# A weight gradient with seven products per pair of slices: another form of the seven products, and accumulations that open and close bank by bank

## The chip, the cores and the metric

The kernel runs on one core of a Trainium2 chip. The metric is device time in microseconds (us). Before the change, three runs gave 163.02, 163.23 and 163.38 us; the median is 163.23 us. Five engines matter here: PE multiplies matrices (PEld is its weight load), DVE (VectorE) and ACT (ScalarE) copy and add, POOL (GpSimd) issues the input transfers, and SP issues the output transfers.

## The reference

```python
batch, m, k, n = 16, 512, 1024, 768
grad_weight = np.einsum('bmk,bmn->kn', input, grad_output)   # float32, 1024 x 768
```

The sum runs over 8192 rows. The kernel cuts them into 64 slices of 128 rows. A slice of the input (128 x 1024) and the same slice of the gradient (128 x 768) give a contribution to all 1024 x 768 outputs.

## The kernel before

**Plain slices.** The output is cut into quarters A, B (input columns 0 to 511) and C, D (columns 512 to 1023), each with one half of the 768 gradient columns. A quarter has four blocks q of 128 x 384, and a block fills one PSUM bank. A plain slice takes 4 x 4 = 16 matmuls of 128 x 128 by 128 x 384.

**Pairs with seven products.** Two adjacent slices can be seen as a 2 x 2 by 2 x 2 block product, which a scheme of Strassen's kind does with seven block products in place of eight: 28 matmuls for a pair in place of 32. For it DVE forms sums and differences of the slices in bf16 first. The string `LOADS` (line 11) says which of the 32 pairs is plain (`s`) and which takes seven products (`P`): seven plain pairs first, then 23, then two plain ones.

The five functions `sum_g1`, `sum_g2`, `sum_x1`, `sum_x2`, `sum_x3` (lines 133 to 158) form the sums of a pair on 1152, 768, 1024, 512 and 1024 columns. Of the seven products two go straight to the quarters A and D; the other five (m, n, o, p, q) have accumulators of their own in `macc` (line 80). At the end `share` (line 179) adds `macc` to the quarters in `acc`: 20 operations on DVE, named by `SHARES`.

**Order of the work.** The engines' orders are written out by hand: `manual_schedule` keeps the program's order on PE, DVE, ACT and POOL. `ORDER` (line 17) lists visits to a quarter or product; a visit takes all four blocks together, in four banks (0 to 3 or 4 to 7), over some slices, and `!` closes it. When a visit opens, ACT may copy the old partial sum from SBUF back into some of its banks (`carry`, line 297). When it closes, `shut` (line 349) either lets ACT copy the bank out (line 354), for blocks that were carried or are new, or lets DVE add the bank to the sum in SBUF (line 358). A number ahead of a step, or behind its `!`, says how many operations of the list `filler` (the sums of the pairs, then the shares) DVE does there.

**Transfers.** POOL issues the loads, which turn float32 into bf16 on the way: one transfer of each operand per pair from pair 2 on (`MERGED = 2`, lines 114 and 115), one per slice before that (lines 119 and 121). 14 pairs are held in SBUF, and sums of 9 pairs. Slices 0 and 1 of the input and slice 0 of the gradient come as float32 and are rounded by DVE and ACT (`round_by`, line 212).

**The end.** The last block is multiplied in two parts, of 256 and 128 columns, in two banks (line 393), each added (line 401) and stored (line 403) by itself.

Of the kernel before, what the change touches and what calls it, by code (L numbers as in the profile page):

```python
# [9 lines left out]
P = 128  # L10

LOADS = "sssssssPPPPPPPPPPPPPPPPPPPPPPPss"
# [5 lines left out]
ORDER = (  # L18
    "A1:3!0,0,0,0 C1:1 B1:3 B2!0,0,0,0 C2!0,0,0,0 D2:3 A2 D3 A3 D4!0,0,0,0 A4 B4:1^!0,0,0,0 C4 "
    "C6!0,0,0,0 A6!0,0,0,0 D6:2~!0,0,0,0 B6:3^ C8!0,0,0,0 B8!0,0,0,0 D8:2~!0,0,0,0 A8!0,0,0,0 "  # L20
    "D9:2 B10!0,0,0,0 D10!0,0,0,0 A10 B12:2^!0,0,0,0 A12!0,0,0,0 D12:3 B14!0,0,0,0 D14!0,0,0,0 "
    "C13:3^ C14!6,0,0,0 A15:1 1o2:4!1,1,1,0 q2:4!0,1,0,1 A16!0,0,0,0 D16:1^ p3:4!2,1,1,0 "
    "D17!0,0,0,0 n3:2 1o4:3!2,0,0,1 n4!0,0,0,0 m4:4!1,1,1,2 p5:1^!0,0,0,0 A19:3^!0,0,0,1 q4:4~ "
    "2q6!2,0,1,0 D20!1,0,0,0 o7:4~!0,1,1,1 n7:2^!1,0,0,1 m7:1^!1,0,0,0 p8:1~ 2A22:4!2,1,0,2 "
    "p9!0,0,0,0 D23:3~!0,0,1,0 q9:3^ 2q10!2,0,0,0 o10:2^!1,0,0,0 n10:2^ 2n11!2,0,0,0 "
    "A25:4~!1,0,1,0 m10:2^ 2m12!2,0,0,0 D26!1,0,0,0 p13:4~!0,1,2,1 o13:3~!0,0,1,1 q12:3~ "
    "2A28:2~!2,0,0,1 q13!0,0,0,0 n15:3~!2,0,1,1 D28:1^!0,0,1,0 o16:2^!0,0,0,0 q16:2~!2,0,0,1 "
    "m15:3~ 1p17:3^!4,0,1,1 D30!1,0,0,0 m16 m18!0,0,0,0 q18:4~!1,1,0,1 A32 1n19:4^!4,0,1,2 "
    "o20:1~!0,1,0,0 D34:3^ 4D35!1,0,0,0 A35!1,0,0,0 o22:2^ p21:4 5p23!1,0,1,1 o23!0,0,0,0 q21:2~ "
    "q23!3,0,0,0 m21:4~ m23!2,1,0,0 n21:4~ A38:0-q n23!5,0,0,1 A40 B18:4!2,1,0,1 A41!0,0,0,0 "  # L30
    "C17:3 C18!1,0,0,0 D41!3,0,0,0 "
# [3 lines left out]
SHARES = (  # L35
    "l20 l21 l22 t20 t21 t22 t10 t11 t12 t13 l23 t23 l10 l11 l12 l13 l30 l31 l32 l33 "
).split()

WARMUP = [("b", 512), ("f", 512), ("f", 512), ("b", 512)]
PAIRS_HELD = 14  # L40
SUMS_HELD = 9

MERGED = 2
# [3 lines left out]
def kernel(  # L47
# [12 lines left out]
    S = B * M // P  # L60
# [4 lines left out]

    LEFT, RIGHT = slice(NH, N), slice(0, NH)
# [10 lines left out]

    acc = accp.tile([P, 2 * Q, N], f32, name="acc")

    macc = accp.tile([P, 5, Q, NH], f32, name="macc")  # L80
    SLOT = {"n": 0, "p": 1, "m": 2, "o": 3, "q": 4}
# [10 lines left out]

# [14 lines left out]
    xg = []  # L107
    for u, kind in enumerate(LOADS):
# [7 lines left out]
        for h in range(2):  # L116
            s = 2 * u + h
            if s > 0 and u < MERGED:
                nc.gpsimd.dma_start(out=gp[:, h, :], in_=G[s * P : (s + 1) * P, :])
            if s > 1 and u < MERGED:  # L120
                nc.gpsimd.dma_start(out=xp[:, h, :], in_=X[s * P : (s + 1) * P, :])
            if kind == "s":
                items.append(("s", xp[:, h, :], gp[:, h, :]))
        if kind == "P":
            items.append(("P", xp, gp))
        xg.append((xp, gp))

    opened = {}
# [4 lines left out]
    def sum_g1(i):  # L133
        _, xp, gp = items[i]
        ge = sums.tile([P, 3, NH], bf16, name="ge")
        xe = sums.tile([P, 3, KH], bf16, name="xe")
        extra[i] = (xe, ge)
        g = gp.rearrange("p m n -> p (m n)")
        nc.vector.tensor_add(out=ge.rearrange("p a n -> p (a n)"), in0=g[:, 0 : 3 * NH], in1=g[:, NH : 4 * NH])  # L139

    def sum_g2(i):
        _, xp, gp = items[i]
        g = gp.rearrange("p m (h n) -> p (m h) n", h=2)
        nc.vector.tensor_sub(out=g[:, 0::3, :], in0=g[:, 0::3, :], in1=g[:, 2:0:-1, :])  # L144

    def sum_x1(i):
        _, xp, gp = items[i]
        xe = extra[i][0]
        nc.vector.tensor_add(out=xe[:, 0:2, :].rearrange("p a k -> p (a k)"), in0=xp[:, 0, :], in1=xp[:, 1, :])  # L149

    def sum_x2(i):
        _, xp, gp = items[i]
        nc.vector.tensor_add(out=extra[i][0][:, 2, :], in0=xp[:, 0, 0:KH], in1=xp[:, 1, KH:K])  # L153

    def sum_x3(i):
        _, xp, gp = items[i]
        x = xp.rearrange("p m (h k) -> p (m h) k", h=2)
        nc.vector.tensor_sub(out=x[:, 1:3, :], in0=x[:, 1:3, :], in1=x[:, 0::3, :])  # L158

    def settled(quarter, q):  # L160
        for p, (_, banks) in opened.items():
            assert p != quarter or not (banks[q][1] and banks[q][2])
        assert not any(b == q and steps[m][1] == quarter for m, b in filled)

    SHARE_OF = {
        "t1": ("m", "o", 0),
        "t2": ("p", "q", 0),
        "t3": ("q", None, 0),  # L170
        "l1": ("n", "m", Q),
        "l2": ("p", "o", Q),
        "l3": (None, "n", Q),
    }
    taken = set()

    def share(name, q):
        left, right, row = SHARE_OF[name]
        sides = [
            (h, p)  # L180
            for h, p in enumerate((left, right))
            if p and ("ABCD"[(row > 0) * 2 + h], p) not in taken
        ]
        for h, _ in sides:
            settled("ABCD"[(row > 0) * 2 + h], q)
        if len(sides) == 2:
            a, b = SLOT[left], SLOT[right]
            dst = acc[:, row + q, :].rearrange("p (h n) -> p h n", h=2)
            src = macc[:, a : b + 1 : b - a, q, :]
        else:  # L190
            ((h, p),) = sides
            dst = acc[:, row + q, h * NH : (h + 1) * NH]
            src = macc[:, SLOT[p], q, :]
        op = nc.vector.tensor_sub if name[1] == "3" else nc.vector.tensor_add
        op(out=dst, in0=dst, in1=src)  # L195

    filler = []
    for i, item in enumerate(items):
        if item[0] == "P":
            filler += [(f, i) for f in (sum_g1, sum_g2, sum_x1, sum_x2, sum_x3)]  # L200
    filler += [(partial(share, c[:2]), int(c[2:])) for c in SHARES]
    filler.reverse()

    def fill(n):
        for _ in range(n):
            f, i = filler.pop()
            f(i)


    def round_by(engine, dst, src, c0, c1):  # L210
# [4 lines left out]
    round_by("DVE", g0, gf, NH, NH + 192)  # L215
    round_by("ACT", g0, gf, NH + 192, N)
# [4 lines left out]
    round_by("ACT", x0, xf[0], 6 * P, 8 * P)  # L221


    KINDS = {"A": "sP", "B": "s", "C": "s", "D": "sP"}
    streams = {
        p: [i for i, item in enumerate(items) if item[0] in KINDS.get(p, "P")] for p in "ABCDmnopq"
    }

    def operands(p, i, q):
        kind, x, g = items[i]  # L230
        k = slice(q * P, (q + 1) * P)
        k2 = slice(KH + q * P, KH + (q + 1) * P)
        left, right = LEFT, RIGHT
        if kind == "s":
            return x[:, k if p in "AB" else k2], g[:, left if p in "AC" else right]
        xe, ge = extra[i]
        return {
            "m": lambda: (xe[:, 2, k], ge[:, 1, :]),
            "n": lambda: (xe[:, 1, k], g[:, 0, left]),
            "o": lambda: (x[:, 0, k], g[:, 0, right]),  # L240
            "p": lambda: (x[:, 1, k2], g[:, 1, left]),
            "q": lambda: (xe[:, 0, k], g[:, 1, right]),
            "D": lambda: (x[:, 0, k2], ge[:, 0, :]),
            "A": lambda: (x[:, 1, k], ge[:, 2, :]),
        }[p]()

    def sum_of(p, q):
        if p in SLOT:
            return macc[:, SLOT[p], q, :]
        row = q if p in "AB" else Q + q  # L250
        return acc[:, row, 0:NH] if p in "AC" else acc[:, row, NH:N]

    done = {p: 0 for p in streams}
    fresh = {p: True for p in streams}
    slots = [0, 1]
    used = set()
# [3 lines left out]
    def parsed(step):  # L260
        step, _, ahead = step.partition("!")
        step, _, byact = step.partition(":")
        early = byact[-1:] if byact[-1:] in ("^", "~") else ""
        byact = byact.rstrip("^~")
        at = next(c for c in step if c.isalpha())
        before, upto = step.split(at)
        ahead = [int(a) for a in ahead.split(",")] if ahead else None
        return int(before or 0), at, int(upto), int(byact[:1] or 0), byact[1:], early, ahead

    steps = [parsed(step) for step in ORDER]  # L270


    def follower(n, free):
        now = {p for p in opened if p != steps[n][1]}
        shut_since = {steps[n][1]}
        for m in range(n + 1, len(steps)):
            _, p, _, byact, first, early, ahead = steps[m]
            if p not in now:
                if not free:
                    if not early:  # L280
                        return None
                    assert byact and not first and not fresh[p] and p not in shut_since
                    return m
                free -= 1
# [168 lines left out]
```

## Time and profile before

| what | us |
|---|---|
| median of three runs | 163.23 |
| span of the profiled execution, first to last instruction | 161.1 |
| PE busy | 157.0 |
| DVE busy | 140.7 |
| ACT busy | 117.9 |
| first matmul of the slices starts | 5.00 |
| last DVE addition ends | 158.1 |

The profile gives no time for its execution but the span; the median of the runs is 2.1 us longer than the span, and this remainder (launch, and landing of the last store) lies around it. PE's granted clock is full in all of the span. The busy time of an engine is the union of its instructions' durations; instructions of DVE and ACT overlap a little, so an engine's pace is read from one start to the next. In the profile's groups, a line like "L358 DVE TENSOR_TENSOR acc<-bank,acc" names the source line, the engine, what is written and read, the count, the busy time and the mean duration of one.

### The profile page before, as it was taken

Reading aid. Unit: us, or ns where it says so; the run is one execution under the profiler, and the core shown is the slowest. Engines: PE = TensorE matmul, PEld = TensorE weight load, DVE = VectorE, ACT = ScalarE, POOL = GpSimd, SP = SyncE. Lnnn points to the kernel's source line nnn. Section 1 sums busy time; section 2 is a strip of 40 time slices with the busy share of each in tenths; the row PEclk is TensorE's granted clock in tenths of the full one; section 3 lists DMA queues with packets and bytes.
Section 4 is the critical chain, followed back from the end, with each engine's and each line's share of the span. In section 5 each row is a group of like instructions: output and inputs, shape, how many; then the busy total and the mean of one; then the engine's idle time right before and its main releaser. Section 6 shows DMA issues by size and latency. Waiting matters only on the chain.

```text
span 161.1 us, 2769 instructions
## 1 busy us (share of the span) xinstructions
PE 157.0 (97%) x944; PEld 92.7 (58%) x944; DVE 140.7 (87%) x267; ACT 117.9 (73%) x278; POOL 34.8 (22%) x69
## 2 busy tenths in 40 slices
PE   8999999999999999999999999999999999999991
PEld 3365665556555565556655665556655665555561
DVE  0645888889799999999998999999989998999982
ACT  3735357545589899978998897997795667988730
POOL 7442222122222212222212222221222100000000
PEclk9999999999999999999999999999999999999999
DMA  5999999999999999999999999999999999900695
GB/s 176 297 210 214 213 214 216 212 215 212 214 213 212 212 212 216 212 213 211 214 212 217 212 215 213 213 213 213 213 212 213 213 214 213 202 21 0 239 354 191
DMA packets 12398, 33.40 MB, mean 207 GB/s; under 512 B 1376, under 2 KB 4192, under 8 KB 12384
## 3 DMA queue, kind: packets, MB, share of 16 engines
q0 software_dynamic: 9360, 28.64, 89.8%
q1 hardware_dynamic: 2592, 3.47, 6.2%
q10 hardware_dynamic: 432, 1.11, 1.8%
q8 instruction: 7, 0.11, 0.3%
q14 instruction: 7, 0.06, 0.1%
HBM read 58.72 MB, written 3.15 MB: 384 GB/s over the span
## 4 chain that ended last, share of the span: by engine, by line
PE 97%; DVE 0%; issue 0%
PE bank L338 94%; PE bank L97 3%; PE bank L393 0%; DVE acc L401 0%
## 5 line engine op out<-in xcount | busy, mean ns | idle before, releaser
L338 PEld LDWEIGHTS <-xp 128*128 128x128 bf16 x650 | 63.3, 98 | 44.4 <-DVE xp L212 1.5
L338 PE MATMUL bank<-gp,xp 128*128 128x384 bf16 x468 | 81.0, 327 | 0.0
L354 ACT COPY macc<-bank 128x384 f32<-128x384 f32 x91 | 39.3, 491 | 9.8 <-PE bank L338 9.4
L358 DVE TENSOR_TENSOR acc<-bank,acc 128x384 f32<-128x384 f32 x80 | 39.6, 550 | 5.2 <-PE bank L338 4.8
L338 PEld LDWEIGHTS <-xe 128*128 128x128 bf16 x276 | 26.9, 98 | 17.9 <-DVE xe L149 0.2
L354 ACT COPY acc<-bank 128x384 f32<-128x384 f32 x57 | 24.7, 484 | 13.9 <-PE bank L338 13.9
L297 ACT COPY bank<-macc 128x384 f32<-128x384 f32 x73 | 33.0, 493 | 1.6 <-DVE acc L358 0.9
L338 PE MATMUL bank<-ge,xp 128*128 128x384 bf16 x182 | 33.5, 326 | 0.0
L338 PE MATMUL bank<-gp,xe 128*128 128x384 bf16 x184 | 32.4, 326 | 0.0
L297 ACT COPY bank<-acc 128x384 f32<-128x384 f32 x47 | 21.5, 491 | 8.7 <-DVE acc L358 7.0
L115 POOL DMA_DIRECT2D xp<-in_input_dram x30 | 16.0, 532 | 52.1 <-DMA xp<-in_input_dram 28.9
L114 POOL DMA_DIRECT2D gp<-in_grad_output_dram x30 | 16.0, 533 | 38.1 <-PE bank L338 17.2
L358 DVE TENSOR_TENSOR macc<-bank,macc 128x384 f32<-128x384 f32 x35 | 18.0, 550 | 0.8 <-PE bank L338 0.8
L139 DVE TENSOR_TENSOR ge<-gp 128x1152 bf16<-128x1152 bf16 x23 | 17.3, 752 | 0.6 <-DMA gp<-in_grad_output_dram 0.5
L149 DVE TENSOR_TENSOR xe<-xp 128x1024 bf16<-128x1024 bf16 x23 | 15.8, 685 | 2.1 <-DMA xp<-in_input_dram 2.1
L195 DVE TENSOR_TENSOR acc<-acc,macc 128x768 f32<-128x768 f32 (+1 forms) x20 | 16.1, 871 | 0.0
L338 PE MATMUL bank<-ge,xe 128*128 128x384 bf16 x92 | 15.9, 326 | 0.0
L158 DVE TENSOR_TENSOR xp<-xp 128x1024 bf16<-128x1024 bf16 x23 | 15.7, 684 | 0.0
L144 DVE TENSOR_TENSOR gp<-gp 128x768 bf16<-128x768 bf16 x23 | 12.7, 554 | 0.5
L153 DVE TENSOR_TENSOR xe<-xp 128x512 bf16<-128x512 bf16 x23 | 9.6, 418 | 0.0
L356 DVE COPY acc<-bank 128x384 f32<-128x384 f32 x6 | 3.2, 555 | 3.2 <-PE bank L338 3.1
L212 DVE CAST gp<-gf 128x192 bf16<-128x192 f32 (+1 forms) x2 | 0.7, 330 | 4.3 <-DMA gf<-in_grad_output_dram 4.3
(20 smaller groups left out, 19.9 us busy)
## 6 DMA issues: line engine op xcount, KB each, us to landing
xp<-in_input_dram POOLq DMA_DIRECT2D x30, 512.0 KB, 16.8
gp<-in_grad_output_dram POOLq DMA_DIRECT2D x30, 384.0 KB, 16.7
out_dram<-acc SPq DMA_DIRECT2D x15, 192.0 KB, 2.4
xf<-in_input_dram ACTq DMA_DIRECT2D x2, 512.0 KB, 4.8
gp<-in_grad_output_dram POOLq DMA_DIRECT2D x3, 192.0 KB, 6.4
xp<-in_input_dram POOLq DMA_DIRECT2D x2, 256.0 KB, 7.7
gf<-in_grad_output_dram SPq DMA_DIRECT2D x2, 192.0 KB, 4.2
out_dram<-acc SPq DMA_DIRECT2D x1, 128.0 KB, 1.9
```

Source lines behind the costliest of these rows:

```text
L114: nc.gpsimd.dma_start(out=gp, in_=G[rows, :].rearrange("(p m) n -> p m n", m=2))
L115: nc.gpsimd.dma_start(out=xp, in_=X[rows, :].rearrange("(p m) k -> p m k", m=2))
L139: nc.vector.tensor_add(out=ge.rearrange("p a n -> p (a n)"), in0=g[:, 0 : 3 * NH], in1=g[:, NH : 4 * NH])
L144: nc.vector.tensor_sub(out=g[:, 0::3, :], in0=g[:, 0::3, :], in1=g[:, 2:0:-1, :])
L149: nc.vector.tensor_add(out=xe[:, 0:2, :].rearrange("p a k -> p (a k)"), in0=xp[:, 0, :], in1=xp[:, 1, :])
L153: nc.vector.tensor_add(out=extra[i][0][:, 2, :], in0=xp[:, 0, 0:KH], in1=xp[:, 1, KH:K])
L158: nc.vector.tensor_sub(out=x[:, 1:3, :], in0=x[:, 1:3, :], in1=x[:, 0::3, :])
L195: op(out=dst, in0=dst, in1=src)
L297: nc.scalar.copy(out=bank, in_=sum_of(p, q))
L338: nc.tensor.matmul(bank, stat, mov, start=opening and j == 0 and not carried, stop=close and j == len(items_now) - 1, skip_group_check=car ...
L354: nc.scalar.copy(out=dst, in_=bank)
L358: nc.vector.tensor_add(out=dst, in0=bank, in1=dst)
```

## The change

- `LOADS`: six plain pairs, then 25 pairs with seven products, then one plain pair.
- The form of the seven products: the sums of a pair are chained. For the input, stage 0 writes two differences (1024 columns), stage 1 takes one of them less a raw half (512), stage 2 adds another raw half to that (512, in place). The gradient has the like on 768, 384 and 384 columns. One product of a pair goes straight to each of A, B and C; four (1, 5, 6, 7) have accumulators in `macc`.
- `SHARES` and `share` go. The accumulators are added as the last blocks close (`close`): 6 takes 1, 7 takes 6, 5 is used twice, and A, B, C and D take one accumulator each, all on DVE from the bank.
- `ORDER` is replaced by `PLAN`, whose unit is one block, not four: `A2@1.3` multiplies block 2 of A over 3 more items, opening bank 1; `f` lets ACT copy the old sum into a bank; `c` closes a block with ACT's copy; `v` closes it with DVE, by an addition or, if the bank was filled, a copy; `x0.6` or `g2.6` is a stage of pair 6's sums.
- Blocks 0 and 1 of A and of C keep banks 0, 3, 4 and 5 from the first slice to the end. All other blocks take turns in banks 1, 2, 6 and 7.
- `MERGED = 3`: slices 4 and 5 are loaded by single transfers. `SUMS_HELD` goes from 9 to 10.

The instruction orders count: 930 matmuls of the slices, 918 of them of 384 columns and 12 parts (before: 938, 926 and 12); on DVE 137 additions of 384 columns from a bank, 24 copies from a bank and 4 + 4 closings of product 5 (before: 115, 8 and none); on ACT 105 copies out of a bank and 124 + 2 into one (before: 148 and 120 + 4).

```diff
-LOADS = "sssssssPPPPPPPPPPPPPPPPPPPPPPPss"
+LOADS = "ssssssPPPPPPPPPPPPPPPPPPPPPPPPPs"
...
+PLAN = (
+    "A0@0.1 A2@1.1 A3@2.1 A1@3.1 vA2 C2@6.1 cA3 C3@7.1 C0@4.1 r0 cC2 C1@5.1 vC3 B0@1.1 B1@2.1 B2@6.1 cB0 "
...
+    "11@1.2 c13 g0.28 11.2 53@7.4 f60@6 v11 70@2.1 g1.28 f61@1 70.3 v53 60.1 g2.28 60.3 v70 61.2 x0.28 "
...
+    "51.5 v73 f53@2 fC3@5 70.3 v51 fD1@0 53.3 fB1@6 C3.3 v70 f50@3 C0.2 v53 fD3@1 B1.7 vC3 fB3@2 50.4 vC0 "
+    "vB1 B3.4 v50 fD0@4 72.1 fB0@5 D1.2 D3.2 vB3 B0.7 v72 f52@3 fC2@6 vD1 52.4 vD3 vB0 C2.6 v52 fD2@0 "
+    "fB2@1+2 D0.2 vC2 D2.2 B2.6 vD0 vD2 vB2 "
 ).split()
-SUMS_HELD = 9
-MERGED = 2
+SUMS_HELD = 10
+MERGED = 3
...
-    macc = accp.tile([P, 5, Q, NH], f32, name="macc")
-    SLOT = {"n": 0, "p": 1, "m": 2, "o": 3, "q": 4}
+    macc = accp.tile([P, 4, Q, NH], f32, name="macc")
+    SLOT = {"1": 0, "5": 1, "6": 2, "7": 3}
...
+    def sum_x(stage, u):
+        x = tiles[u][0].rearrange("p m (h k) -> p (m h) k", h=2)
+        xe = sums_of(u)[0]
+        if stage == 0:
+            nc.vector.tensor_sub(out=xe[:, 0:2, :], in0=x[:, 1::-1, :], in1=x[:, 3::-2, :])
+        elif stage == 1:
+            nc.vector.tensor_sub(out=xe[:, 2, :], in0=xe[:, 0, :], in1=x[:, 0, :])
+        else:
+            nc.vector.tensor_add(out=x[:, 1, :], in0=x[:, 2, :], in1=xe[:, 2, :])
+
+    def sum_g(stage, u):
+        g = tiles[u][1].rearrange("p m (h n) -> p (m h) n", h=2)
+        ge = sums_of(u)[1]
+        if stage == 0:
+            nc.vector.tensor_add(out=ge[:, 0:2, :], in0=g[:, 0:2, :], in1=g[:, 1::2, :])
+        elif stage == 1:
+            nc.vector.tensor_add(out=ge[:, 2, :], in0=g[:, 3, :], in1=ge[:, 0, :])
+        else:
+            nc.vector.tensor_add(out=g[:, 1, :], in0=ge[:, 2, :], in1=g[:, 2, :])
...
+            "B": lambda: (x[:, 1, k], g[:, 3, :]),
+            "C": lambda: (x[:, 3, k], g[:, 1, :]),
+            "5": lambda: (xe[:, 0, k], ge[:, 0, :]),
+            "6": lambda: (xe[:, 2, k], ge[:, 2, :]),
+            "7": lambda: (xe[:, 1, k], ge[:, 1, :]),
...
+    SHARED = {"A": "1", "B": "5", "C": "7", "D": "6", "6": "1", "7": "6"}
...
+    def fill(p, q, b, b2):
...
+        for tile_, c0, c1 in parts:
+            nc.scalar.copy(out=tile_[:, 0 : c1 - c0], in_=src[:, c0:c1])
+        opened[p, q] = (parts, True)
...
+    def close(engine, p, q):
+        parts, carried = opened.pop((p, q))
+        final = done[p, q] == len(streams[p])
+        dst = sum_of(p, q)
+        if final and p not in "1":
...
+                if p == "5":
+                    nc.vector.tensor_sub(out=dst, in0=b, in1=sum_of("6", q))
+                    nc.vector.tensor_sub(out=sum_of("6", q), in0=b, in1=sum_of("7", q))
                 else:
+                    nc.vector.tensor_add(out=dst[:, c0:c1], in0=b, in1=sum_of(SHARED[p], q)[:, c0:c1])
+                if p in "ABCD":
...
+                    store.dma_start(out=OUT[:, row, at : at + c1 - c0], in_=dst[:, c0:c1])
...
+            if engine == "c":
+                nc.scalar.copy(out=dst, in_=b)
+            elif carried or fresh[p, q]:
+                nc.vector.tensor_copy(out=dst, in_=b)
             else:
+                nc.vector.tensor_add(out=dst, in0=b, in1=dst)
```

## The prediction

> **What bounds the kernel now.** The first view is the busy time of each engine, with the slices of the span under it.
>
> ```profile
> PE 157.0 (97%) x944; PEld 92.7 (58%) x944; DVE 140.7 (87%) x267; ACT 117.9 (73%) x278; POOL 34.8 (22%) x69
> ...
> PE   8999999999999999999999999999999999999991
> ...
> DVE  0645888889799999999998999999989998999982
> ACT  3735357545589899978998897997795667988730
> ...
> PEclk9999999999999999999999999999999999999999
> DMA  5999999999999999999999999999999999900695
> ```
>
> PE works without a hole at full clock, so time is matmuls times their pace. But DVE is full in most slices too, and the transfers are full until about slice 35 of 40: three resources run side by side with little air. The chain of the work that ended last confirms PE and gives its pace:
>
> ```profile
> 0.78 4.42 PE bank L97 x6
> 5.20 2.25 PE bank L338 x12
> 7.45 0.01 issue
> 7.46 149.34 PE bank L338 x914
> ...
> 156.79 0.67 PE bank L393 x6
> 157.46 0.02 issue
> 157.49 0.63 DVE acc L401 x2
> ```
>
> 914 matmuls in 149.34 us are 0.163 us each. The end is PE's last part and two additions, to 158.12; the store follows.
>
> The third view is DVE's timeline in a full stretch, since its durations overlap: the pace is read from start to start.
>
> ```profile
> 59.43 0.75 DVE L139 TENSOR_TENSOR ge<-gp 128x1152 bf16<-128x1152 bf16 x1
> 60.21 0.56 DVE L144 TENSOR_TENSOR gp<-gp 128x768 bf16<-128x768 bf16 x1
> 60.69 0.68 DVE L149 TENSOR_TENSOR xe<-xp 128x1024 bf16<-128x1024 bf16 x1
> 61.29 0.42 DVE L153 TENSOR_TENSOR xe<-xp 128x512 bf16<-128x512 bf16 x1
> 61.62 0.68 DVE L158 TENSOR_TENSOR xp<-xp 128x1024 bf16<-128x1024 bf16 x1
> 62.23 0.75 DVE L139 TENSOR_TENSOR ge<-gp 128x1152 bf16<-128x1152 bf16 x1
> 63.01 0.56 DVE L144 TENSOR_TENSOR gp<-gp 128x768 bf16<-128x768 bf16 x1
> 63.49 1.95 DVE L358 TENSOR_TENSOR acc<-bank,acc 128x384 f32<-128x384 f32 x4
> ```
>
> Paces: 768 columns of bf16 0.48 us, 1024 0.60, 512 0.33; an addition from a bank (1.95 - 0.55) / 3 = 0.467. An operation usually starts 0.08 before the one ahead ends (60.69 + 0.68 against 61.29), but L144, which overwrites what L139 reads, starts 0.03 after its end: a dependent operation directly behind its producer loses 0.11.
>
> **The change, part by part.**
>
> *Matmuls.* Before: 926 of 384 columns and the last block's 12 parts, worth 932; after: 918 and 12 parts, worth 924. Two more pairs with seven products save 4 each: 8 x 0.163 = **-1.30 us**, on the path.
>
> *DVE, in total.* The sums of a pair cost 0.78 + 0.48 + 0.60 + 0.33 + 0.61 = 2.80 before. After: 1024, 512, 512, 768, 384 and 384 columns, 0.60 + 0.33 + 0.33 + 0.48 + 2 x 0.27 = 2.28. The 384 form is in no row; it lies between 0.27 (the line through 512 and 1024 columns, 0.33 - 0.067) and 0.33 (as 512). I take 0.27, since 768 columns fit the same line (0.47 against 0.48). 23 x 2.80 = 64.4 becomes 25 x 2.28 = 57.0: -7.4. The shares go (16 x 0.87 + 4 x 0.47, from 0.951 and 0.550 less the overlap): -15.8. Closings with 384 columns go from 115 + 8 to 137 + 24 + 8 = 169: 46 x 0.467 = +21.5. In the new order 28 stages stand directly behind the stage they read and 4 closings of product 5 behind their twin: 32 x 0.11 = +3.5. Sum +1.8 us of DVE, 142.5 of about 160: no cost by itself, if its place is right.
>
> *DVE, by stretch.* From the first sum of pair 6 (matmul 165 in the new order) to the first sum of pair 24 (matmul 640) PE needs 475 x 0.163 = 77.4 us. DVE has 18 x 2.28 + 72 closings x 0.467 + 18 direct dependences x 0.11 = 76.6, or 99%. I take nothing for it: each single pair's share lies between 0.93 and 1.02, and the old kernel's DVE was as full at 50 to 80 us without PE waiting. With the 384 form at 0.33 it would be 78.8.
>
> On this the Trainium skill, "VectorE: DVE Perf Modes", has two rules against each other and against the change. Its section "The TRN2 errata" says each operation pays a fixed extra, so operands of 512 columns and more are better; the 50 new stages of 384 columns go against that. Its "Rules for kernel authors" tell that waits between chained operations cost nothing and only the count matters; the trace shows 0.11 for L144. By the second rule the 32 dependences would be free and DVE's sum -1.7 instead of +1.8; the trace decides.
>
> *ACT.* 148 copies out and 124 fills become 105 and 126. At about 0.38 and 0.42 each that is -16.3 + 0.8 = -15.5 us; ACT has air already, so 0.
>
> *Banks.* Four banks are held by A and C, four take turns. Counted in the instruction orders, the median distance from a block's last matmul to the next block's first in the same bank falls from 15 to 11 matmuls where DVE closes, 15 to 8 where ACT does, and from 19 to 14 and 12 with a fill; the smallest are 6, 4, 10 and 9. The rows price the chain: matmul 0.327, DVE 0.550 or ACT 0.491, a fill 0.49. So DVE needs 0.88 us (5.4 matmuls), ACT 0.82 (5.0), with fills 1.37 and 1.31 (8.4 and 8.0), and hand-offs of about 0.05 each. Only the one distance of 4, early in slice 0, is too short: +0.2. Everything else fits if a closing starts at once; a closing that stands behind a 0.60 sum does not. I take +0.2, with 0 to 3 as its bounds.
>
> *Transfers.* Single transfers add two issues on POOL (0.56 each against 0.53), in a time when POOL waits 2.0 anyway: 0. Single slices landed 2.25 apart (9.49 and 11.74), a merged pair 4.29 after (16.03); four singles in place of two merged ones make all later landings up to 0.2 late. In the new order each pair's first matmul comes within 0.7 us of its landing in the old trace, so PE follows the transfers throughout. The last input landed at 142.2; 83 matmuls' worth follow its first use, so PE cannot end before 142.2 + 13.5 + 0.2 = 155.9 (it ended at 157.8). That caps the gain at 1.9 us, or 1.7 with the late landings. Taken: 0 beyond the matmuls.
>
> *The end.* From the closing of A2 (its last matmul is 844) DVE has 29 operations: 27 x 0.467 + 0.34 + 0.29 + 4 x 0.11 + the matmul's own 0.36 = 14.0 us. PE needs 74 x 0.163 + 1.16 (the parts, 156.63 to 157.79) = 13.2. DVE ends 0.8 after PE, in place of 0.33 (158.12 - 157.79): **+0.5**. Stores start 13 us before the end, earlier than now, and cost nothing; the last store follows the same two additions.
>
> Sum: -1.3 + 0.2 + 0.5 = -0.6 on a span of 161.1, 160.5; with the 2.1 us around it, **162.6 us**.
>
> **Rivals.**
>
> *DVE becomes the bound of the pair stage (slower).* For: 99% of an in-order queue, and distances that leave a closing 1 to 3 matmuls of air. It decides from the point at which DVE's work in the stretch passes 77.4 us: at 0.33 for the 384 form it is 78.8, +1.4, and landings that DVE waited for before can no longer be made up:
>
> ```profile
> DVE xe L149 <- DMA xp<-in_input_dram: 2.1, 4, 0.8
> ...
> DVE ge L139 <- DMA gp<-in_grad_output_dram: 0.5, 2, 0.2
> ```
>
> Those are 2.6 more. 162.6 + 1.4 + 2.6 gives up to 166.6, about 165 in the middle. Against: the sums' paces lie on a line, and closings lie spread among the sums.
>
> *The gain is eaten at the end and by small waits (no change).* 29 closings in a row, fills behind them, and PE waiting for both: another 0.6 gives 163.2.
>
> *The floor of the transfers is met.* If the start loses nothing and DVE keeps up at the end, PE ends at 156.1 and the time is 163.23 - 1.7 = 161.5.
>
> **How the numbers follow.** Forecast, 162.6 (its own range 162.1 to 162.9): 0.43. Floor, 161.5 to 162.1: 0.13. No change, 162.9 to 163.55: 0.15. DVE-bound, 163.55 to 167: 0.29. About 0.2% (0.33 us) is what a measurement of this kernel can tell from no change. So faster 0.56, same 0.15, slower 0.29. Leaving out the lowest 0.05 and the highest 0.1, the range is 161.7 to 165.8.
>
> **What would show it.** Right: PE's matmuls worth 924 at 0.163; idle of PE's weight load put down to DVE and ACT below 1 us in all; DVE's 384 stages at a mean of about 0.35 each (0.27 and the overlap); after 143 us DVE without gaps, its last addition 0.8 us after PE's last matmul. The rival shows as idle of the weight loads spread over 35 to 110 us, put down to DVE's sums or to the filled banks, with DVE full. The prediction fails if transfers land later than before by more than 0.2 us, or if closings on DVE wait behind sums.

## The result and the profile after

The changed kernel takes 162.77 us (median of 11 runs, 162.70 to 162.91), the kernel before 163.02 us beside it (11 runs). The ratio is 0.9979 with a 95% interval of 0.9971 to 0.9987: faster by about 0.34 us, a quarter of what the eight matmuls' worth of PE time would give.

The page of the changed kernel: the engines' busy time, and PE, DVE, ACT and the transfers in 40 slices.

```profile
span 161.0 us, 2767 instructions
...
PE 155.2 (96%) x936; PEld 92.1 (57%) x936; DVE 144.2 (90%) x328; ACT 107.1 (67%) x237; POOL 35.7 (22%) x71
...
PE   8899999999999999999999999999999999999990
...
DVE  0789978688999999999999999999999899989991
ACT  3653765887879878677977777577736632797530
...
PEclk9999999999999999999999999999999999999999
DMA  4999999999999999999999999999999999916455
```

The clock is full in all slices, as before. PE is busy 1.8 us less and still has no hole to be seen; the transfers end in the same slices; DVE gained 3.5 us, ACT lost 10.8. The span fell by 0.17 us only. The chain that ended last, in order of time, shows where PE's part of it stops (columns: start, length, what).

```profile
39.20 117.37 PE bank L286 x726
156.56 0.05 DVE acc L310
156.61 0.09 issue
156.70 0.73 DVEq L374
157.43 0.20 DVE acc L310
```

PE's last matmul ends at 156.55 us, 1.24 us earlier than before, close to the matmuls' price of 1.30. Behind it the chain now stays on DVE for 1.08 us (157.63); before it was 0.33. So the gain arrived at PE and was given back at the end. The whole account, from the two profiled executions:

| stretch | before | after | difference |
|---|---|---|---|
| span's start to the first matmul of the slices | 5.00 | 5.17 | +0.18 |
| from there to the end of PE's last matmul | 152.79 | 151.38 | -1.41 |
| from there to the end of DVE's last addition | 0.33 | 1.08 | +0.75 |
| from there to the landing of the last store | 1.91 | 2.16 | +0.26 |
| from there to the span's end | 1.10 | 1.16 | +0.06 |

DVE's timeline at the end of the changed kernel (start, length, line, operation; the bracket tells an idle time ahead and what ended it):

```profile
146.41 0.56 DVE L310 TENSOR_TENSOR macc<-bank,macc 128x384 f32<-128x384 f32 x1
147.22 0.56 DVE L306 TENSOR_TENSOR macc<-bank,macc 128x384 f32<-128x384 f32 x1 [0.26 <-PE bank L286]
147.81 0.56 DVE L307 TENSOR_TENSOR macc<-bank,macc 128x384 f32<-128x384 f32 x1
148.28 0.55 DVE L310 TENSOR_TENSOR macc<-bank,macc 128x384 f32<-128x384 f32 x1
148.75 0.55 DVE L306 TENSOR_TENSOR macc<-bank,macc 128x384 f32<-128x384 f32 x1
149.33 0.56 DVE L307 TENSOR_TENSOR macc<-bank,macc 128x384 f32<-128x384 f32 x1
...
154.57 0.55 DVE L306 TENSOR_TENSOR macc<-bank,macc 128x384 f32<-128x384 f32 x1
155.15 0.56 DVE L307 TENSOR_TENSOR macc<-bank,macc 128x384 f32<-128x384 f32 x1
155.63 2.00 DVE L310 TENSOR_TENSOR acc<-bank,macc 128x384 f32<-128x384 f32 x5
```

From 147.22 on no bracket follows: DVE is never again idle for long enough to be listed. The first difference of product 5 (L306) reads an accumulator that the second (L307) overwrites, and L307 starts 0.58 to 0.59 after L306, where other closings follow at 0.465 to 0.47. That is the 0.11 of a direct dependence, four times. Two explanations compete. **Theory 1:** PE kept the whole saving, and this row of closings, with the stores bunched behind it, gave about 1 us back. **Rival 2:** the gain was lost in the stage of the pairs, where DVE is full and banks turn over tightly, and the end only shows it.

### The profile page after: what moved, and what is told of

Read it like the earlier page. It is cut to its first block, busy times and chain, and to the rows that moved or that the text cites. A ratio compares the mean times of both kernels' runs of the same rounds, so it can differ in the third digit from the quotient of the medians.

```text
span 161.0 us, 2767 instructions
## 1 busy us (share of the span) xinstructions
PE 155.2 (96%) x936; PEld 92.1 (57%) x936; DVE 144.2 (90%) x328; ACT 107.1 (67%) x237; POOL 35.7 (22%) x71
## 4 chain that ended last, share of the span: by engine, by line
PE 91%; DMA 3%; DVE 1%; ACT 1%; DVEq 0%; issue 0%; SPq 0%; ACTq 0%
PE bank L286 91%; DMA gf<-in_grad_output_dram 3%; DVE acc L325 1%; ACT acc L321 1%; DVEq L374 0%; ACT bank L273 0%; SPq L127 0%; DVE gp L201 0%; DVE gp L197 0%; DVE ge L195 0%; DVE acc L310 0%; ACTq L321 0%
## 5 line engine op out<-in xcount | busy, mean ns | idle before, releaser
L286 PE MATMUL bank<-gp,xp 128*128 128x384 bf16 (+1 forms) x630 | 110.6, 324 | 0.6 <-ACT xp L201 0.3
L286 PE MATMUL bank<-ge,xe 128*128 128x384 bf16 x300 | 57.1, 326 | 0.0
L273 ACT COPY bank<-acc 128x384 f32<-128x384 f32 (+2 forms) x63 | 29.3, 478 | 12.1 <-DVE acc L325 5.6
L321 ACT COPY acc<-bank 128x384 f32<-128x384 f32 x50 | 23.9, 479 | 15.5 <-PE bank L286 14.9
L321 ACT COPY macc<-bank 128x384 f32<-128x384 f32 x55 | 26.0, 479 | 11.0 <-PE bank L286 10.7
L325 DVE TENSOR_TENSOR macc<-bank,macc 128x384 f32<-128x384 f32 x50 | 27.3, 550 | 0.1
L193 DVE TENSOR_TENSOR ge<-gp 128x768 bf16<-128x768 bf16 x25 | 13.7, 550 | 1.2 <-DMA gp<-in_grad_output_dram 1.2
L187 DVE TENSOR_TENSOR xp<-xp,xe 128x512 bf16<-128x512 bf16 x25 | 10.5, 418 | 0.4
L185 DVE TENSOR_TENSOR xe<-xe,xp 128x512 bf16<-128x512 bf16 x25 | 10.4, 416 | 0.2
L195 DVE TENSOR_TENSOR ge<-gp,ge 128x384 bf16<-128x384 bf16 x25 | 8.7, 349 | 0.2
L197 DVE TENSOR_TENSOR gp<-ge,gp 128x384 bf16<-128x384 bf16 x25 | 8.7, 349 | 0.2
```

Source lines behind the costliest of these rows:

```text
L185: nc.vector.tensor_sub(out=xe[:, 2, :], in0=xe[:, 0, :], in1=x[:, 0, :])
L187: nc.vector.tensor_add(out=x[:, 1, :], in0=x[:, 2, :], in1=xe[:, 2, :])
L193: nc.vector.tensor_add(out=ge[:, 0:2, :], in0=g[:, 0:2, :], in1=g[:, 1::2, :])
L195: nc.vector.tensor_add(out=ge[:, 2, :], in0=g[:, 3, :], in1=ge[:, 0, :])
L273: nc.scalar.copy(out=tile_[:, 0 : c1 - c0], in_=src[:, c0:c1])
L286: nc.tensor.matmul(tile_[:, 0 : c1 - c0], stat, mov[:, c0:c1], start=first and j == 0, stop=True, skip_group_check=True,)
```

## The experiments

Ratios are against the kernel before, on the same chip; the median in brackets is this kernel's.

**1. Less work on DVE at the end.** The second subtraction of product 5's closings is left out.

```diff
                     nc.vector.tensor_sub(out=dst, in0=b, in1=sum_of("6", q))
-                    nc.vector.tensor_sub(out=sum_of("6", q), in0=b, in1=sum_of("7", q))
```

> The changed kernel without the second subtraction of product 5's closings (four DVE operations near the end), so quarter D gets a wrong accumulator. Theory 1 (PE kept the whole 1.3 us of the matmuls; DVE's row of closings at the end, which runs without a hole from 147.2 us and ends 1.08 us after PE's last matmul, and the bunched last stores gave about 1 us back): 4 x (0.467 + 0.115) = 2.3 us of DVE go, so DVE's last addition falls back to about 0.33 us behind PE's last matmul, and the time falls by 0.7 to 1.0 us, to a ratio of 0.992 to 0.994 against the kernel before. Rival 2 (the gain was lost in the pair stage, to full DVE and tight banks): no change against the changed kernel, ratio 0.998.

Measured: ratio 0.9943, 0.9930 to 0.9957 (162.22 us), 0.55 us under the changed kernel. Rival 2 falls: nothing was touched ahead of 147 us. But 2.3 us of DVE bought only 0.55, less than the 0.7 to 1.0 expected; the timeline says why:

```profile
154.06 0.56 DVE L306 TENSOR_TENSOR macc<-bank,macc 128x384 f32<-128x384 f32 x1
155.02 2.02 DVE L309 TENSOR_TENSOR acc<-bank,macc 128x384 f32<-128x384 f32 x5 [0.40 <-PE bank L286]
```

DVE now waits 0.40 for PE ahead of C2's closing, and then five closings stand in a row again, to 0.47 behind PE's last matmul; the last store still lands 2.16 us after that. These five closings are the next limit; whether another order of them helps this kernel was not tried.

**2. The same work without the direct dependence.** Product 1's slot is dead by then; the second difference goes there.

```diff
-    SHARED = {"A": "1", "B": "5", "C": "7", "D": "6", "6": "1", "7": "6"}
+    SHARED = {"A": "1", "B": "5", "C": "7", "D": "1", "6": "1", "7": "6"}
...
-                    nc.vector.tensor_sub(out=sum_of("6", q), in0=b, in1=sum_of("7", q))
+                    nc.vector.tensor_sub(out=sum_of("1", q), in0=b, in1=sum_of("7", q))
```

> The changed kernel, with product 5's second difference written to the accumulator slot of product 1, which nothing needs any more, in place of the slot that the first difference has just read; quarter D takes it from there. The four direct dependences (0.115 us each) go, nothing else. Theory 1: DVE's row at the end gets 4 x 0.115 = 0.46 us shorter, and the time falls by about 0.4 us, ratio 0.995. Rival 2: no change, ratio 0.998.

Measured: ratio 0.9942, 0.9930 to 0.9955 (162.25 us): 0.52 us under the changed kernel, with the same number of operations. The timeline of this kernel:

```profile
147.14 0.56 DVE L306 TENSOR_TENSOR macc<-bank,macc 128x384 f32<-128x384 f32 x1 [0.26 <-PE bank L286]
147.62 0.55 DVE L307 TENSOR_TENSOR macc<-bank,macc 128x384 f32<-128x384 f32 x1
148.08 0.55 DVE L310 TENSOR_TENSOR macc<-bank,macc 128x384 f32<-128x384 f32 x1
...
154.59 0.55 DVE L307 TENSOR_TENSOR macc<-bank,macc 128x384 f32<-128x384 f32 x1
155.05 2.01 DVE L310 TENSOR_TENSOR acc<-bank,macc 128x384 f32<-128x384 f32 x5
```

L307 now follows L306 by 0.464 to 0.474. The row starts 0.08 earlier than in the changed kernel, its last five closings 0.58 earlier; the last addition ends at 157.06 in place of 157.63. The four waits, 0.46 us in all, had reached the end of the kernel almost one for one: PE's end moved by 0.07, the stretch from there to DVE's last addition fell by 0.50, and the stores took as long as before.

**3. Slices 4 and 5 in merged transfers again.**

```diff
-MERGED = 3
+MERGED = 2
```

> The changed kernel with slices 4 and 5 in one transfer per operand again. The first matmul of slice 4 comes at about 14.5 us in the changed kernel and would have to wait for 16.0, so PE loses up to 1.5 us there, but later transfers land up to 0.2 us sooner. Theory 1: since PE then runs late against the landings, the slack with later landings lets it keep the loss: time up by 0.8 to 1.5 us, ratio 1.003 to 1.007. Rival 2 (full DVE sets the pace of the pair stage): PE's late start is partly hidden behind DVE's pace, up by less than 0.5 us.

Measured: ratio 1.0062, 1.0050 to 1.0075 (164.17 us), 1.4 us over the changed kernel. PE's weight loads say where:

```profile
PEld L286 <- DMA xp<-in_input_dram: 1.8, 1, 1.8
```

One wait, for slice 4: that matmul starts at 16.21 us with a hole of 1.55, and PE's end moves from 156.55 to 157.97. Nothing later takes the loss up: neither DVE nor the landings set a later pace of their own behind which the loss could hide. Without the single transfers the change would have been a loss.

**4. Another order in slice 0.**

```diff
-    "r1 B3@7.1 r2 r3 vB1 D0@1.2 r4 A0.1 vB2 A1.1 cB3 D1@2.2 ...
+    "r1 B3@7.1 r2 r3 vB1 r4 A0.1 vB2 A1.1 D0@1.2 cB3 D1@2.2 ...
```

> The changed kernel with D0 of slices 0 and 1 behind A0 and A1 of slice 1, so that the bank that ACT has to empty is used 2 matmuls later. It should remove the 0.24 us hole ahead of the 13th matmul. Theory 1: PE is 0.2 us earlier in the start, but the landings (first use within 0.7 us of landing, one wait of 0.1 us at 138 us) and DVE's row at the end take most of it: between 0 and 0.2 us faster, ratio 0.997 to 0.998. Rival 2: no change.

Measured: ratio 0.9983, 0.9974 to 0.9992 (162.83 us): no change. The hole ahead of matmul 12 is still 0.23 us, now ended by DVE's rounding of slice 1. The bank's wait had only stood in front of another one, of equal length.

**5. The single transfers in the old kernel.** The edit is `MERGED = 2` to `MERGED = 3` in the kernel before.

> The kernel before, with slices 4 and 5 in single transfers and nothing else. In its trace the first matmul of slice 4 came at 16.03 us, at the landing of the merged transfer, with a wait of 0.05 us, and its order visits slices 4 and 5 together. Theory 1: no gain for the old order, ratio 0.999 to 1.001; the single transfers pay only together with an order that uses slice 4 alone. Rival 2 (the later landings cost it): 0.2 us slower, ratio 1.001.

Measured: ratio 1.0011, 1.0001 to 1.0021 (163.11 us): no gain, and rather the 0.1% loss that rival 2 names; between the two the interval hardly decides. The old order cannot use slice 4 alone.

**6. More work on DVE in every pair.** On the kernel of experiment 2.

```diff
+    spare = accp.tile([P, 128], bf16, name="spare")
...
             (sum_x if op == "x" else sum_g)(int(stage), int(u))
+            if op == "g" and stage == "0":
+                nc.vector.tensor_add(out=spare, in0=tiles[int(u)][1][:, 0, 0:128], in1=tiles[int(u)][1][:, 1, 0:128])
```

> The kernel without the wait at the end (162.25 us), with one more DVE operation per pair, an addition of 128 bf16 columns that nothing reads, about 0.13 us from start to start, behind the pair's first gradient sum. From pair 6 to 23 DVE's work goes from 76.6 to 79.0 us where PE needs 77.4. Theory 1 with the working of the prediction (DVE at 99%, without air): PE falls behind by 1.5 to 3 us, time 163.7 to 165, ratio 1.003 to 1.012. Rival (DVE's fullness is work done ahead, with air in it): under 0.3 us, ratio 0.994 to 0.996.

Measured: ratio 1.0041, 1.0027 to 1.0055 (163.63 us), 1.4 us over experiment 2 by the medians and 1.6 by the ratios, for 25 operations that each take 0.135 from start to start, 3.4 us of DVE. Not all of that is added, though: in five pairs the new operation stands between two gradient sums of which the second reads the first, and so removes a dependence of 0.115. The net is 2.8 us, and 2.0 between pairs 6 and 23, where the expectation counted 2.4. PE's busy time by stretches of this kernel (us, then PE, PEld, DVE, ACT, POOL busy with counts, clock, transfers' share, GB/s) and the waits of its weight loads:

```profile
40.00:60.00 20.00, 19.91 (x122) 11.58 (x121) 19.93 (x52) 16.58 (x39) 4.75 (x9) 1.00 1.07 213
60.00:80.00 20.00, 19.96 (x122) 11.65 (x121) 20.00 (x53) 14.87 (x34) 4.83 (x10) 1.00 1.07 214
```

```profile
PEld L288 <- issue: 2.9, 15, 0.3
PEld L288 <- DVE xp L203: 1.6, 2, 1.3
```

The view of the waits names no cause for the fifteen idle times of the weight loads ("issue"). The times of the neighbours name one: PE's holes between 30 and 140 us grow from 0.3 in experiment 2 to 1.75, and twelve of the thirteen between 48 and 115 us end 0.04 after DVE closed, or ACT refilled, a bank that the next matmul waits for; the last one ends behind one of DVE's sums. One of the twelve:

```profile
78.10 0.55 DVE L327 TENSOR_TENSOR macc<-bank,macc 128x384 f32<-128x384 f32 x1
78.70 0.97 PE L288 MATMUL bank<-ge,xe 128*128 128x384 bf16 x5
```

In this execution, the slowest of the six, PE's end moved to 158.34. So the prediction's 99% was the edge: DVE is not the bound of the pair stage as the change stands, but 2.0 us more between pairs 6 and 23 push 1.4 of it onto PE. By these two numbers the air is about 0.6 us, an estimate from one trace.

**7. D0 ahead of C2, on the kernel of experiment 2.**

```diff
-    ... 52.4 vD3 vB0 C2.6 v52 fD2@0 "
-    "fB2@1+2 D0.2 vC2 D2.2 B2.6 vD0 vD2 vB2 "
+    ... 52.4 vD3 vB0 D0.2 C2.6 v52 fD2@0 "
+    "fB2@1+2 vD0 vC2 D2.2 B2.6 vD2 vB2 "
```

> The kernel without the wait at the end, with D0's two last matmuls ahead of C2's last six, and its closing ahead of C2's. In the trace without the wait DVE stands idle 0.4 us ahead of C2's closing and then does C2, D0, D2 and the two parts of B2 in a row, ending 0.5 us to 0.6 us after PE. Theory 1: D0 fills the idle time, the row ends 0.1 to 0.2 us earlier and the last stores are less bunched: 0.1 to 0.3 us faster than 162.25, ratio 0.992 to 0.994. Rival: PE's end alone counts, no change.

Measured: ratio 0.9951, 0.9939 to 0.9963 (162.23 us): no change against 162.25 that the intervals can tell. The expectation misread its own trace: the idle 0.40 belongs to experiment 1. In experiment 2 the row runs without a hole through product 5's second differences, and an order inside a full row moves nothing. DVE's end stays 0.58 behind PE's in both.

**8. A hole in the middle, and a landing.** On the kernel of experiment 7.

```diff
-    ... A2.1 g2.7 fC3@1 A0.1 10@7.1 vB2 A1.1 ...
+    ... A2.1 fC3@1 A0.1 10@7.1 vB2 g2.7 A1.1 ...
...
-    ... 13@1.1 g2.30 13.2 x0.30 f12@6 11.3 v13 12.3 ...
+    ... 13@1.1 g2.30 13.1 x0.30 f12@6 11.2 13.1 11.1 v13 12.3 ...
```

> The kernel with D0 earlier, with two more moves: the third gradient sum of pair 7 behind the closing of B2 (the hole of 0.22 us ahead of matmul 204, where that closing came late), and the third matmul of 13, the first to need pair 30, two places later (PE waits there for its landing, 0.04 to 0.19 us). Theory 1: PE ends 0.2 us earlier, so 0.2 us faster than with D0 earlier, ratio 0.991 to 0.993. Rival: another landing or closing takes over, no change.

Measured: ratio 0.9960, 0.9946 to 0.9973 (162.39 us): no gain. The hole of 0.22 ahead of matmul 204 became three of 0.08, 0.12 and 0.04; the wait for pair 30 went, and the last pair's landing took its place (0.12 ahead of matmul 841, behind 0.07 for a refill by ACT ahead of 833). PE ends at 156.63, against 156.58 in experiment 7. Here the rival is right: PE runs so close behind the landings that in this trace a hole removed ahead of 140 us came back as a wait there.

**9 and 10. Four operations fewer in DVE's last row, and nothing left out.** Quarter D continues in product 5's bank, and product 7's accumulator is taken off D's sum in SBUF beforehand, in experiment 9 by POOL and in experiment 10, for comparison, by DVE; D0 stands ahead of C2 as in experiment 7.

```diff
                 if p == "5":
                     nc.vector.tensor_sub(out=dst, in0=b, in1=sum_of("6", q))
-                    nc.vector.tensor_sub(out=sum_of("6", q), in0=b, in1=sum_of("7", q))
+                    opened["D", q] = (parts, True)
+                elif p == "D":
+                    nc.vector.tensor_add(out=dst, in0=b, in1=dst)
...
+        elif op == "s":
+            q = int(rest)
+            nc.gpsimd.tensor_sub(out=sum_of("D", q), in0=sum_of("D", q), in1=sum_of("7", q))
```

In `PLAN` the four fills of D go, `s1 s3`, `s0` and `s2` stand behind the closings of 73, 70 and 72, and the last blocks of 50, B3 and 52 move to banks 0, 1 and 4.

> The end of the changed kernel in another form: quarter D's last matmuls continue in the bank of product 5 behind its one remaining closing, and POOL, which is idle then, takes product 7's accumulator off D's sum in SBUF beforehand. Four DVE operations, four direct dependences and four fills of ACT go; D0's matmuls come ahead of C2's, as in the run before. Theory 1: DVE's row gets air, its last addition falls from 0.58 us (without the wait at the end) to about 0.33 us behind PE's last matmul, the last stores are less bunched: 161.8 to 162.1 us, ratio 0.992 to 0.994 at best 0.99. Rival: POOL's four subtractions slow DVE's row down or come late (no row of this case shows POOL adding), then 162.3 us or more.

> The same with the four subtractions on DVE instead of POOL, so DVE has as many operations at the end as the kernel without the wait (162.25 us), only ACT's four fills are fewer. Theory 1 (the count of DVE's operations in its last row sets the end): as the kernel without the wait, 162.2 to 162.4 us, and slower than with POOL by 0.1 to 0.4. Rival: the four fills of ACT mattered, then as fast as with POOL.

Measured: with POOL 0.9920, 0.9907 to 0.9934 (161.91 us); with DVE 0.9939, 0.9926 to 0.9951 (162.26 us). The two differ in nothing but the engine of four subtractions, and by 0.35 us; the one with DVE equals experiment 2, whose last row has as many operations (22 from 147.1 us on), though ACT has four fills less. So DVE's work in its last row is what counts. POOL's group, and the end of DVE's timeline, with POOL's help:

```profile
L346 POOL TENSOR_TENSOR acc<-acc,macc 128x384 f32<-128x384 f32 x4 | 4.0, 996 | 23.2 <-DVE macc L312 23.2
```

```profile
154.59 0.55 DVE L309 TENSOR_TENSOR acc<-bank,acc 128x384 f32<-128x384 f32 x1
155.40 0.56 DVE L312 TENSOR_TENSOR acc<-bank,macc 128x384 f32<-128x384 f32 x1 [0.26 <-issue]
155.87 0.55 DVE L309 TENSOR_TENSOR acc<-bank,acc 128x384 f32<-128x384 f32 x1
156.38 0.64 DVE L312 TENSOR_TENSOR acc<-bank,macc 128x256 f32<-128x256 f32 x2
```

D0's closing starts at 154.59, ahead of the wait; behind PE's last matmul (156.62) DVE needs 0.40. The last store lands 1.96 us after, in place of 2.16. With the four subtractions on DVE (L346):

```profile
152.37 0.55 DVE L312 TENSOR_TENSOR macc<-bank,macc 128x384 f32<-128x384 f32 x1
152.95 0.56 DVE L346 TENSOR_TENSOR acc<-acc,macc 128x384 f32<-128x384 f32 x1
153.42 1.01 DVE L309 TENSOR_TENSOR acc<-bank,acc 128x384 f32<-128x384 f32 x2
...
156.68 0.61 DVE L312 TENSOR_TENSOR acc<-bank,macc 128x256 f32<-128x256 f32 x2
```

The row is full again from 147.12 us on, two of the subtractions start 0.58 behind the closing that they read, and DVE ends at 157.29, against 157.02 with POOL's help. The stretch behind PE's last matmul is 0.40 here too, since PE itself ends 0.28 later: 0.11 of that is a wait for a DVE closing ahead of matmul 916, and 0.10 a landing at 138.7. So in these two traces POOL's help shows in PE's end and in the stores (1.96 against 2.14), not in the additions behind PE as the expectation had it. The version with POOL beats both kernels, by 1.3 us against the one before.

## Why the prediction was right, and where not

It forecast 162.6 us, a gain of 0.6, and the kernel gained 0.25 (medians) to 0.34 (ratio), on the side it named and inside its range. That is about the 0.33 us which the prediction called the least that can be told from no change. The total also owes something to luck, since misses of its terms cancel in part: the end cost 0.5 more than priced, while the banks' 0.2 did not come and PE's holes gave 0.1.

- **Matmuls, -1.30:** right. From the first matmul to the last PE took 1.41 less: 1.31 for the matmuls and 0.10 for holes (time from start to start beyond the usual 0.163: 1.17 us before, 1.07 after).
- **DVE and ACT in total, +1.8 and -15.5:** their busy times changed by +3.5 and -10.8. The sums counted every operation at its pace in a row; more of them now stand alone and count with their full duration (on DVE 65 in place of 46, on ACT 140 in place of 76). Neither was on the path, as said.
- **DVE by stretch, 0:** right, and by the right price. The 384 form takes 0.265 from start to start, the low end taken; a stage directly behind its producer loses 0.115. PE's holes between 30 and 140 us sum to about 0.4. Experiment 6 shows how near the slower rival was: 2.0 us more of DVE there cost about 1.4. The bound of 0.33 for the 384 form (78.8 in place of 76.6) would have been such an error.
- **Banks, +0.2:** the hole ahead of matmul 12 came as counted, 0.24, but it cost nothing new: the old kernel had 0.17 there, and experiment 4 found the rounding of slice 1 behind it. Past 12 us PE waited noticeably for a bank twice, 0.07 ahead of matmul 75 and 0.22 ahead of matmul 204, both for a closing on DVE.
- **Transfers, 0:** no landing held PE up by more than 0.1 us, but the part was priced too low as a help: the single transfers are worth 1.4 us to this order (experiment 3). Landings were late as said, 0.21 at slice 5 (16.24 against 16.03), but 0.54 at the last pair (142.76 against 142.21). More than 0.2 was to be a sign that the prediction fails; PE paid only 0.1 us for it, at pair 30.
- **The end, +0.5:** the mechanism was right, the size was off. It cost 1.0: 0.75 on DVE and 0.26 in the stores. Two sentences failed. The row was counted as unbroken from A2's closing; DVE in fact ran out of work once more, 0.26 us ahead of product 5's first closing, so the row started later. And "stores cost nothing" looked at their start; the last four of 384 and 256 columns are issued 0.465 us apart, and the last landed 2.16 us after DVE's end in place of 1.91.

One more of its signs did not come: the idle time of the weight loads put down to DVE is 1.8 us, not below 1. Of this 1.6 is the rounding of the first slices, which cost 1.5 before.

The table's +0.18 in the first row is hardly the new order's: the profiled execution of experiment 5, in the old order, started its matmuls at 5.18 as well, and in both the first input slice landed later (4.74 and 4.87 against 4.65). In all other traces of this case they start between 5.17 and 5.21, so the early start is that of one execution of the kernel before. Since its cause was not tried apart, it stays open; so does why the next to last pair's input takes 0.3 to 0.4 us more than its neighbours in the changed kernel and in experiment 3 alike (4.66 and 4.73 against 4.31), while the old order with single transfers shows 4.32.

## What to carry to other kernels

When work is taken off a full engine, follow the last stage engine by engine to the last store: the saving is worth only what the slowest of the engines behind it lets through, and there each operation counts from start to start, dependences included. An engine that is busy 99% need not be the bound, as here; a small operation added to each round tells how much air it has. Look for dead buffers: writing to one instead of the place that the neighbour has just read cost nothing and was worth more than the whole change.

## What the runs showed of the hardware

- Two neighbouring DVE operations where the second overwrites an operand of the first start 0.58 to 0.59 us apart, and 0.46 to 0.47 if it writes elsewhere (128 x 384 float32, the changed kernel and experiment 2). The Trainium skill, "VectorE: DVE Perf Modes", section "Rules for kernel authors", advises for chained operations to keep down their count, not their semaphores; experiment 2 has the same count and is 0.52 us faster. The measurement decides.
- POOL takes 1.00 us for a subtraction of 128 x 384 in float32 in SBUF, against 0.55 to 0.56 for the same on DVE (experiments 9 and 10), and DVE's closings beside it kept their 0.55 to 0.56.
- The changed kernel's last stores on SP, issued 0.465 us apart, landed 0.43 to 0.58 apart, and its very last store took 2.13 us from issue to landing, against 1.87 before. That the burst is the cause fits this, but was not tried apart.
